# Attention's output product by Strassen's method, with the low parts of its summed weights made by accumulating DMA

## The chip, the cores and the metric

The kernel runs on one core of one Trainium2 chip, as one program. The metric is the device time of one execution in microseconds (us). Before the change the median of three runs is 1040.52 us (1040.29 to 1040.53).

## What is computed

One decoder layer on 512 tokens of width 1024, in float32: a gated feed-forward part, a token mixer, cross-attention into 256 memory tokens, and a second gated feed-forward part, each followed by `x <- LN(alpha*x + sublayer(x))`. The change is in the third, cut here to what matters:

```python
def _memory_attention(h, mem, wq, wk, wv, wo):
    q = (h @ wq).reshape(b_, s_, XA_HEADS, XA_HEAD_DIM)      # 4 heads of 256
    k = (mem @ wk).reshape(b_, m_, XA_HEADS, XA_HEAD_DIM)
    v = (mem @ wv).reshape(b_, m_, XA_HEADS, XA_HEAD_DIM)
    s = jnp.einsum('bshd,bmhd->bhsm', q, k).astype(jnp.float32) * (XA_HEAD_DIM ** -0.5)
    p = jax.nn.softmax(s, axis=-1).astype(v.dtype)
    o = jnp.einsum('bhsm,bmhd->bshd', p, v).reshape(b_, s_, D_MODEL)
    return o @ wo                                            # 512x1024 @ 1024x1024
h = _layernorm(ALPHA * h + _memory_attention(...), ln3_g[l], ln3_b[l])
```

## The kernel before

Every float32 product is made of three matmuls on halves of the numbers: a tile is split into `hi` (a cast on ACT, L67) and `lo` (a subtraction on DVE, L68; the helper is `split`), and hi*hi, hi*lo and lo*hi are added up in PSUM. A weight block of 128 x 1024 (512 KB) is loaded by SP into `raw_...`, split into `whi_...` and `wlo_...` (helper `wblock`; kept blocks are called `ws_...`), and used by all token tiles.

The two feed-forward parts use Strassen's method: 7 products of half-sized matrices instead of 8. The sums of activations that it needs are made on DVE, and those of weights, t1 to t4, by DMA in scratch memory ahead of time: POOL issues a plain copy (L281) and then an accumulating DMA (L290). These are put on a list (`todo_behind`) and issued one at a time behind weight blocks as they come by (`one_behind`: a tiny POOL operation `seen`, L322, reads the new block, and the DMA follows it), at a rate set by `pace`; in the second feed-forward part four at a time behind `seen` at L307. POOL also computes the reciprocal root of each layer-norm (`rstd`, L174).

The attention runs head by head: `xq` projects the queries (tiles `pxq`, split to `q`), `scores` makes `sc`, from which DVE takes the maximum (`mx`, L950) and ACT the exponentials (`e`, L956), DVE scales them (L961), `attend` transposes them on TensorE (`pt`) and splits them (`PT`), and `values` multiplies by the memory's values (`po`) and splits the result (`oT`).

The output product with `wo` is the ordinary one: `out_gemm` (named "xo") takes the output's two halves of 512 columns in turn. For each half, each token tile and each of 8 blocks of 128 inputs there are 3 matmuls of 128x512 (L223 to L225, into `xops`): 2 x 4 x 8 x 3 = 192. Each half is added to `h` (L240), with statistics (L243); after the second half a tile is normalised (`ln_tile`, L166 to L180) and transposed on TensorE (`transpose_h`, into `trh`, split to `xoT`, copied to `y`). The second feed-forward part starts with two ordinary column blocks (`f2p`, L56 to L58, from weights `f2g` and `f2u`), and goes on with Strassen products; its first is `f2w` at L547.

The order of each engine's instructions is made by the framework's scheduler from the program, and is fixed when the kernel is built; semaphores make an engine wait for its inputs.

Of the kernel before, what the change touches and what calls it, by code (L numbers as in the profile page):

```python
# [9 lines left out]
F32 = mybir.dt.float32  # L10
# [6 lines left out]
P = 128  # L17
S = 512
# [16 lines left out]
def layer_kernel(ctx: ExitStack, tc: tile.TileContext, a, out):  # L35
# [35 lines left out]
    def wblock(src, name, stay=False):  # L71
        n = src.shape[-1]
        raw = raw4([P, n], f"raw_{name}")
        nc.sync.dma_start(raw, src)
        if stay:
            both = b8([P, 2, n], F32R, f"ws_{name}")
            hi, lo = both[:, 0, :], both[:, 1, :]
        else:
            hi, lo = q4([P, n], f"whi_{name}"), q4([P, n], f"wlo_{name}")
        split(raw, hi, lo)  # L80
        one_behind(hi)
        return hi, lo
# [183 lines left out]
    class Sums:  # L266


        def __init__(self, wsrc, name, kb1, kb2):
            self.w, self.name, self.kb1, self.kb2, self.T = wsrc, name, kb1, kb2, {}  # L270
            self.copies = [(p, b) for some in (("t1", "t3", "t2"), ("t4",)) for b in range(len(kb1)) for p in some]
            self.adds = list(self.copies)

# [51 lines left out]
    def strassen_gemm(groups, S_, alpha, g, b, eps, name, final=False, pre=None, ys=None):  # L325
# [61 lines left out]
        if len(groups) == 1:  # L387
            quarter_["s1"] = [raw4([P, 4, 256], f"{name}s1")]
        else:
            s1 = b8([P, 2, 4, 256], F32, f"{name}s1")  # L390
            s1_ = [sm.tile([P, n, 256], F32, tag="s1", name=f"{name}s1_{n}", bufs=2) for n in (2, 1)]
            quarter_["s1"] = [s1[:, 0], s1[:, 1], *s1_]
# [61 lines left out]
        return [(tiles[k // 2][:, k % 2, 0, :], tiles[k // 2][:, k % 2, 1, :]) for k in range(KT)]  # L454

# [212 lines left out]
    T0 = b8([P, H * S], F32, "T0")  # L668
    pf01 = proj_T2(wf, X1, "pf")
# [7 lines left out]
    sums2 = Sums(a["w2out"], "f2", *FFN_BLOCKS)  # L677
    todo_behind += sums2.actions()
    pace[:] = 0, 2, 3
# [248 lines left out]
    Q, PP, OT = {}, {}, {}  # L928
# [45 lines left out]
    def values(hd, PT):  # L974
        oT = b8([P, 2, 2, S], F32R, f"oT{hd}")
        for j in range(2):
            po = mm_ps("po")
            csl = slice((2 * hd + j) * P, (2 * hd + j + 1) * P)
            for m in range(2):
                mm3(po, VM[m][:, 0, csl], VM[m][:, 1, csl], PT[:, m, 0, :], PT[:, m, 1, :], m == 0, m == 1)  # L980
            split(po, oT[:, j, 0, :], oT[:, j, 1, :])
        OT[hd] = oT
# [8 lines left out]
    xq(3)  # L991
    p1 = attend(1)
# [7 lines left out]
    X3 = out_gemm(a["wo"], KT, lambda k: (OT[k // 2][:, k % 2, 0, :], OT[k // 2][:, k % 2, 1, :]),  # L1000
                  ALPHA, a["ln3_g"], a["ln3_b"], LN_EPS, "xo", ys=ys,
                  pre=lambda: wx.extend(wblock(a["w2in"][u * FT], f"f2{'gu'[u]}0") for u in range(2)))
# [76 lines left out]
```

## Time and profile before

| | before |
|---|---|
| median of 3 runs | 1040.52 us (1040.29 to 1040.53) |
| the profiled execution, its own time | 1040.28 us |
| its span, first to last instruction | 1038.5 us |
| TensorE (PE) busy | 1024.5 us, 99% |
| PE's weight loads (PEld) | 926.9 us, 89% |
| VectorE (DVE) | 830.7 us, 80% |
| ScalarE (ACT) | 508.3 us, 49% |
| GpSimd (POOL) | 137.4 us, 13% |
| clock granted to TensorE, mean | 0.996 of full speed |

All times below are in us from the span's start. PE's busy time runs to the modelled end of a matmul, which overlaps the next one's start, so the distance of starts tells what a matmul costs.

### The profile page before, as it was taken

What the parts mean: (1) busy time and instruction counts of PE and PEld (TensorE: products, weight loads), DVE (VectorE), ACT (ScalarE), POOL (GpSimd) and SP (SyncE); (2) the same over time, 40 slices, a digit from 0 to 9 for tenths busy, and PEclk for the clock granted to TensorE, in tenths of its full rate; (3) what the DMA queues carried; (4) which work ended last, traced back from release to release, by engine and by line L of the source; (5) the groups of instructions that cost most, each with busy time, mean ns of one, the idle gap of its engine ahead of it and who ended that gap; (6) DMA issues with size and microseconds to landing.
All of it is one profiled execution on the core that took longest, in us unless ns stands there. A gap on an engine that the chain in (4) does not pass through costs nothing. (4 is left out here: it accounts for less than half of the span.)

```text
span 1038.5 us, 17839 instructions
## 1 busy us (share of the span) xinstructions
PE 1024.5 (99%) x6898; PEld 926.9 (89%) x6898; DVE 830.7 (80%) x1360; ACT 508.3 (49%) x879; POOL 137.4 (13%) x212
## 2 busy tenths in 40 slices
PE   9999999999999999999999999999999999999995
PEld 8999999998887988879888988889999999988884
DVE  7999888889989645886686356589988888889885
ACT  5566555566644422235324345236555555565731
POOL 0011111215200101002212100110000000025000
PEclk9999999999999999999999999999999999999998
DMA  9375776578966455544819741603333332359761
GB/s 359 130 243 164 220 230 201 144 232 263 285 212 241 145 155 150 148 128 131 239 60 339 207 110 61 203 23 123 90 104 124 100 102 86 119 178 241 240 236 68
DMA packets 46148, 177.36 MB, mean 171 GB/s; under 512 B 6512, under 2 KB 7792, under 8 KB 42736
## 3 DMA queue, kind: packets, MB, share of 16 engines
q1 hardware_dynamic: 40176, 130.09, 36.3%
q0 software_dynamic: 5888, 46.14, 18.0%
q8 instruction: 54, 0.88, 0.3%
q14 instruction: 30, 0.25, 0.1%
HBM read 174.11 MB, written 48.23 MB: 214 GB/s over the span
## 5 line engine op out<-in xcount | busy, mean ns | idle before, releaser
L547 PE MATMUL f2u<-xt,qf2s 128*128 128x256 f32 x480 | 60.7, 283 | 0.0
L547 PE MATMUL f1u<-xt,qf1s 128*128 128x256 f32 x480 | 60.7, 283 | 0.0
L547 PEld LDWEIGHTS f1u<-xt,qf1s 128*128 128x128 f32 x480 | 59.0, 192 | 0.0
L547 PEld LDWEIGHTS f2u<-xt,qf2s 128*128 128x128 f32 x480 | 59.0, 192 | 0.0
L174 POOL TENSOR_TENSOR rstd<-ve,mhalf 128x1 f32<-128x1 f32 x16 | 15.6, 973 | 153.9 <-DVE ve L172 153.9
L68 DVE TENSOR_TENSOR wlo_wv<-raw_wv,whi_wv 128x1024 fp32r<-128x1024 f32 x12 | 14.7, 1224 | 23.4 <-PE pq L57 8.5
L547 PE MATMUL f2w<-xoT,qf2a 128*128 128x256 f32 x240 | 32.1, 284 | 0.0
L547 PE MATMUL f1u<-xT,qf1a 128*128 128x256 f32 x240 | 32.1, 283 | 0.0
L547 PE MATMUL f2u<-xoT,qf2a 128*128 128x256 f32 x240 | 32.1, 283 | 0.0
L547 PE MATMUL f1w<-xT,qf1a 128*128 128x256 f32 x240 | 32.1, 284 | 0.0
L307 POOL TENSOR_TENSOR seen<-qf2a,mhalf 128x1 f32<-128x1 f32 x10 | 5.9, 593 | 188.2 <-ACT qf2a L67 188.2
L547 PE MATMUL f1u<-xt,qf1a 128*128 128x256 f32 x240 | 30.7, 284 | 0.0
L547 PE MATMUL f1v<-xt,qf1s 128*128 128x256 f32 x240 | 30.7, 284 | 0.0
L547 PE MATMUL f2v<-xt,qf2s 128*128 128x256 f32 x240 | 30.4, 284 | 0.0
L547 PE MATMUL f1v<-xT,qf1s 128*128 128x256 f32 x240 | 30.4, 283 | 0.0
L547 PE MATMUL f2v<-xoT,qf2s 128*128 128x256 f32 x240 | 30.4, 284 | 0.0
L547 PE MATMUL f2u<-xt,qf2a 128*128 128x256 f32 x240 | 30.4, 283 | 0.0
L547 PEld LDWEIGHTS f1w<-xT,qf1a 128*128 128x128 f32 x240 | 30.3, 192 | 0.1
L547 PEld LDWEIGHTS f2w<-xoT,qf2a 128*128 128x128 f32 x240 | 30.3, 192 | 0.0
L547 PEld LDWEIGHTS f1u<-xT,qf1a 128*128 128x128 f32 x240 | 30.2, 192 | 0.0
L547 PEld LDWEIGHTS f2u<-xoT,qf2a 128*128 128x128 f32 x240 | 30.2, 192 | 0.0
L547 PEld LDWEIGHTS f1u<-xt,qf1a 128*128 128x128 f32 x240 | 29.6, 192 | 0.1
(435 smaller groups left out, 3305.8 us busy)
## 6 DMA issues: line engine op xcount, KB each, us to landing
f1t<-in_w1out POOLq DMA_DIRECT2D x30, 512.0 KB, 8.0
f2t<-in_w2out POOLq DMA_DIRECT2D x30, 512.0 KB, 6.6
raw_f1t<-f1t SPq DMA_DIRECT2D x20, 512.0 KB, 4.4
raw_f2t<-f2t SPq DMA_DIRECT2D x20, 512.0 KB, 4.9
raw_f2g<-in_w2in SPq DMA_DIRECT2D x17, 512.0 KB, 3.7
raw_f2u<-in_w2in SPq DMA_DIRECT2D x17, 512.0 KB, 3.8
raw_f1u<-in_w1in SPq DMA_DIRECT2D x15, 512.0 KB, 5.9
raw_f1b<-in_w1out SPq DMA_DIRECT2D x15, 512.0 KB, 7.5
```

The lines of the kernel that those rows point to most:

```text
L68: nc.vector.tensor_tensor(out=lo, in0=src, in1=hi.bitcast(F32), op=ALU.subtract)
L174: nc.gpsimd.tensor_tensor(out=rstd, in0=ve, in1=mhalf[:, 0:1], op=ALU.pow)
L307: ins = nc.gpsimd.tensor_tensor(out=seen, in0=q[:, 0, 0:1].bitcast(F32), in1=mhalf[:, 0:1], op=ALU.mult).ins
L547: nc.tensor.matmul(o, q[:, w, wsl], x[k][r], start=opens and k == 0 and n == 0, stop=ends and k == 3 and n == 2, skip_group_check=True)
```

## The change

The output product goes to a new function `strassen_heads`: 7 products of 256 x 512 x 512, so 7 x 24 = 168 matmuls of 128x512 (L496), into the accumulators u, v and w, two tiles each. The inputs are no longer split as they leave `values`: ACT copies `po` as float32 into two tiles `oT` (L1095), which are split a quarter at a time (`left`, 4 x 256 elements; seven such), with four combinations on DVE (`combine`, L481). The weights: three direct quarters b11, b21, b22 (six blocks, split as before) and four sums t1 to t4 (eight blocks, loaded from scratch). For the sums DVE makes no low part: ACT casts the block to hi (L82) and writes -hi into lo (L83), and POOL issues a DMA that accumulates the float32 source into lo (L84). t1 and t2 are loaded and made behind the last queries, t3 and t4 within the product. 14 additions to `h` (L513, L516) stand in place of 8. The scratch sums of `wo` (8 copies and 8 accumulations, `xot`) are put on the list ahead of those for the second feed-forward part (`f2t`), and the list starts with the mixer's f projections; it is stopped while the product runs, so what is left of f2t goes to the steps of the second feed-forward part.

```diff
-    def wblock(src, name, stay=False):
+    def wblock(src, name, stay=False, by_dma=False):
...
-        split(raw, hi, lo)
+        if by_dma:
+
+            nc.scalar.copy(out=hi, in_=raw)
+            nc.scalar.activation(lo, hi.bitcast(F32), AF.Copy, scale=-1.0)
+            nc.gpsimd.dma_start(lo, src, accum_op=ALU.add, max_dma_last_dim=8192)
+        else:
+            split(raw, hi, lo)
         one_behind(hi)
...
+    def sum_blocks(S_, name, *which):
+
+        for p in which:
+            for i in range(2):
+                assert (p, i) in S_.T and (p, i) not in S_.adds
+                S_.ready[p, i] = wblock(S_.T[p, i], f"{name}{p}{i}", True, True)
+
+    def strassen_heads(A1, A2, S_, alpha, g, b, eps, name, ys=None, fill=None, pre=None):
...
+        A["s1"] = raw4([P, 4, 256], f"{name}s1")
+        product(left("a11"), "b11", u, True)
+        combine("s1", "a21", "a22", ALU.subtract)
+        L = left("s1")
+        for t in range(2):
+            add(t, 0, u[t], True)
+        product(L, "t1", v, True)
+        combine("a21", "a11", "a21", ALU.subtract)
+        combine("a11", "s1", "a11", ALU.subtract)
+        L = left("a11")
+        for t in range(2):
+            add(2 + t, 1, v[t], True)
+        product(L, "t2", u)
+        L = left("a12")
+        for t in range(2):
+            add(t, 1, u[t], True, ALU.subtract)
+        product(L, "b21", w, True, True)
+        combine("a12", "a12", "a11", ALU.add)
+        L, L3 = left("a12"), left("a21")
+        for t in range(2):
+            add(t, 0, w[t], False, last=True)
+        B22 = list(right("b22"))
+        sum_blocks(S_, name, "t3", "t4")
+        L4, T3, T4 = left("a22"), list(right("t3")), list(right("t4"))
+        GB = ln_bcast(g, b)
+        for t in by_tiles(L, B22, v, True):
+            add(t, 1, v[t], False, last=True)
+            ln_tile(t, stats[t], GB, eps)
+        for t in by_tiles(L3, T3, u):
+            add(2 + t, 1, u[t], False, ALU.subtract, last=True)
...
+        if fill is None:
+            transpose_h(0, tiles, ys)
+        for t in by_tiles(L4, T4, u, True):
+            if fill is None and t == 0:
+                transpose_h(1, tiles, ys)
+            add(2 + t, 0, u[t], True, last=True)
+            ln_tile(2 + t, stats[2 + t], GB, eps)
+            if t == 0 and pre is not None:
+                pre()
...
+        for t in range(0 if fill is not None else 2, NT):
+            transpose_h(t, tiles, ys)
...
+    sums_xo = Sums(a["wo"], "xo", [0, 1], [2, 3])
+    sums2 = Sums(a["w2out"], "f2", *FFN_BLOCKS)
+    todo_behind += sums_xo.actions() + sums2.actions()
+    pace[:] = 0, 2, 3
     pf01 = proj_T2(wf, X1, "pf")
...
-    sums2 = Sums(a["w2out"], "f2", *FFN_BLOCKS)
-    todo_behind += sums2.actions()
-    pace[:] = 0, 2, 3
...
-            split(po, oT[:, j, 0, :], oT[:, j, 1, :])
-        OT[hd] = oT
+            nc.scalar.copy(out=OT[hd // 2][:, 2 * (hd % 2) + j, :], in_=po)
...
     xq(3)
+    pace[:] = 0, 0, 1
+    sum_blocks(sums_xo, "xo", "t1", "t2")
     p1 = attend(1)
...
-    X3 = out_gemm(a["wo"], KT, lambda k: (OT[k // 2][:, k % 2, 0, :], OT[k // 2][:, k % 2, 1, :]),
-                  ALPHA, a["ln3_g"], a["ln3_b"], LN_EPS, "xo", ys=ys,
-                  pre=lambda: wx.extend(wblock(a["w2in"][u * FT], f"f2{'gu'[u]}0") for u in range(2)))
+    pace[:] = 0, 0, 1
+    X3 = strassen_heads(*OT, sums_xo, ALPHA, a["ln3_g"], a["ln3_b"], LN_EPS, "xo", ys=ys,
+                        pre=lambda: wx.extend(wblock(a["w2in"][u * FT], f"f2{'gu'[u]}0") for u in range(2)))
```

The first place is ACT while the last queries and the softmaxes of heads 2 and 3 run (`q_6553` and `q_6558` are the last head's queries, `PT_6627` and `PT_6652` the transposed weights of head 1). Before, ACT's rows are

```order
L67 CAST oT_6534<-po 128x512 x2
L67 CAST q_6553<-pxq 128x512
L67 CAST whi_xo_2_6894<-raw_xo_2_6892 128x1024
L67 CAST q_6553<-pxq 128x512
L67 CAST PT_6627<-pt 128x512 x2
L67 CAST whi_xo_3_6904<-raw_xo_3_6902 128x1024
L956 ACTIVATE e,sume<-sc,mx 128x256 x4
L67 CAST oT_6688<-po 128x512 x2
```

and after

```order
L1095 COPY oT_6541<-po 128x512 x2
L67 CAST q_6558<-pxq 128x512
L82 CAST ws_xot_6630<-raw_xot_6628 128x1024
L82 CAST ws_xot_6636<-raw_xot_6634 128x1024
L83 ACTIVATE ws_xot_6630<-ws_xot_6630 128x1024
L83 ACTIVATE ws_xot_6636<-ws_xot_6636 128x1024
L82 CAST ws_xot_6642<-raw_xot_6640 128x1024
L82 CAST ws_xot_6648<-raw_xot_6646 128x1024
L67 CAST q_6558<-pxq 128x512
L83 ACTIVATE ws_xot_6642<-ws_xot_6642 128x1024
L83 ACTIVATE ws_xot_6648<-ws_xot_6648 128x1024
```

Two casts of `wo` blocks have gone from here to a later place, and eight passes over summed weights of the same size have come in ahead of the casts of head 1's `PT`, the last two queries' halves among them. Behind this, the three matmuls of the output product that stood between the first two of the last `po` before (L223 to L225) are no longer there on PE.

The second place is PE at the end of the output product, where the tiles are transposed (trh00 and trh01 are the two halves of token tile 0, trh10 and trh11 those of tile 1). Before, around tile 0:

```order
L223 MATMUL xops11_7073<-whi_xo1_3_6988,oT3_6802 128x512
L224 MATMUL xops11_7073<-wlo_xo1_3_6989,oT3_6802 128x512
L192 MATMUL trh00_7057<-ident_262,h0_266 128x128 x4
L225 MATMUL xops11_7073<-whi_xo1_3_6988,oT3_6802 128x512
L192 MATMUL trh01_7065<-ident_262,h0_266 128x128 x4
L223 MATMUL xops11_7073<-whi_xo1_3_6988,oT3_6802 128x512
L224 MATMUL xops11_7073<-wlo_xo1_3_6989,oT3_6802 128x512
L225 MATMUL xops11_7073<-whi_xo1_3_6988,oT3_6802 128x512
```

and after, where tile 1 is transposed (tile 0 stands just ahead of these rows, tiles 2 and 3 further on among the `f2p`):

```order
L496 MATMUL xou0_6842<-ws_xot40_7027,xoa22_7037 128x512 x6
L496 MATMUL xou0_6842<-ws_xot41_7033,xoa22_7037 128x512 x6
L496 MATMUL xou1_6843<-ws_xot40_7027,xoa22_7037 128x512 x6
L496 MATMUL xou1_6843<-ws_xot41_7033,xoa22_7037 128x512 x5
L198 MATMUL trh10_7153<-ident_262,h1_267 128x128 x4
L496 MATMUL xou1_6843<-ws_xot41_7033,xoa22_7037 128x512
L56 MATMUL f2p0_7256<-xoT0_7120,whi_f2g0_7183 128x256
L56 MATMUL f2p1_7257<-xoT0_7120,whi_f2u0_7189 128x256
L56 MATMUL f2p0_7366<-xoT0_7120,whi_f2g1_7356 128x256
L198 MATMUL trh11_7161<-ident_262,h1_267 128x128 x4
```

Before, three of the four tiles are transposed inside the output product, each a tile's matmuls (24) after the one ahead of it; now tile 1's transposes stand at its last matmul and the first `f2p`, and tiles 2 and 3 come in the `f2p`.

The third place is POOL, from the last DMA of the attention to the layer-norm. Before:

```order
L322 TENSOR_TENSOR seen<-ws_xo_1_6974,mhalf 128x1
L281 DMA f2t_6979<-in_w2out 16x8192
L322 TENSOR_TENSOR seen<-whi_xo_3_6988,mhalf 128x1
L290 DMA f2t_6411<-in_w2out 128x512
L322 TENSOR_TENSOR seen<-whi_f2g_7001,mhalf 128x1
L281 DMA f2t_7007<-in_w2out 16x8192
L174 TENSOR_TENSOR rstd<-ve,mhalf 128x1 x4
```

and after:

```order
L297 DMA f2t_6092<-in_w2out 64x2048
L84 DMA ws_xot_6630<-xot_4121 128x1024
L84 DMA ws_xot_6636<-xot_4263 128x1024
L84 DMA ws_xot_6642<-xot_4227 128x1024
L84 DMA ws_xot_6648<-xot_4556 128x1024
L84 DMA ws_xot_7015<-xot_4159 128x1024
L84 DMA ws_xot_7021<-xot_4459 128x1024
L84 DMA ws_xot_7027<-xot_4815 128x1024
L84 DMA ws_xot_7033<-xot_5056 128x1024
L180 TENSOR_TENSOR rstd<-ve,mhalf 128x1 x4
```

Three pairs of `seen` and an f2t DMA (and some ahead of these rows) have moved to the second feed-forward part, and eight accumulating DMAs into SBUF (L84) stand without any `seen` ahead of the four `rstd` of the layer-norm.

## Rows read from the trace of the kernel before

**Rows 1.** The page: busy time of each engine, its share of the span, instructions.

```profile
PE 1024.5 (99%) x6898; PEld 926.9 (89%) x6898; DVE 830.7 (80%) x1360; ACT 508.3 (49%) x879; POOL 137.4 (13%) x212
```

**Rows 2.** The chain that ended last, by engine.

```profile
PE 32%; DVE 1%; DMA 1%; issue 0%; ACT 0%; DVEq 0%
```

**Rows 3.** Windows: busy time of each engine and instructions, granted clock, DMA share, GB/s.

```profile
626.00:644.00 18.00, 17.76 (x113) 15.55 (x112) 12.81 (x31) 10.43 (x28) 0.56 (x2) 1.00 0.25 88
644.00:694.00 50.00, 49.50 (x229) 40.45 (x230) 33.56 (x51) 13.64 (x19) 8.06 (x11) 1.00 0.33 106
694.00:720.00 26.00, 25.97 (x215) 25.57 (x214) 23.92 (x40) 14.49 (x25) 0.99 (x1) 1.00 0.35 123
```

**Rows 4.** One stretch inside the output product, its matmuls alone (same columns).

```profile
648.00:677.00 29.00, 29.00 (x130) 24.03 (x129) 3.43 (x5) 1.00 0.57 182
```

**Rows 5.** Output product's tile: duration min/median/max, first, last start (L224, L225 alike).

```profile
L223 PE MATMUL xops<-whi_xo,oT x40: 388/390/479, 644.4 to 693.2; 128*128 128x512 f32 x40
L223 PE MATMUL xops<-ws_xo,oT x24: 389/390/398, 668.5 to 690.9; 128*128 128x512 f32 x24
```

**Rows 6.** Groups of instructions by form: busy us, mean ns | idle before.

```profile
L68 DVE TENSOR_TENSOR wlo_xo<-raw_xo,whi_xo 128x1024 fp32r<-128x1024 f32 x3 | 3.7, 1226 | 8.0 <-PE xops L224 4.3 <-PE pxq L57 3.7
...
L67 ACT CAST ws_xo<-raw_xo 128x1024 fp32r<-128x1024 f32 x3 | 3.1, 1058 | 0.0
...
L68 DVE TENSOR_TENSOR oT<-po,oT 128x512 fp32r<-128x512 f32 x6 | 3.9, 685 | 1.9 <-ACT oT L67 1.9
...
L240 DVE SCALAR_TENSOR_TENSOR h<-h,xops 128x512 f32<-128x512 f32 x8 | 5.5, 684 | 4.3 <-PE xops L225 4.3
L747 ACT ACTIVATE mg<-pm,psc x4: 692/692/693, 435.6 to 461.2; 128x512 fp32r<-128x512 f32 x4
```

**Rows 7.** Timeline of ACT: start, duration, [idle before it <- what ended it].

```profile
629.55 0.59 ACT L67 CAST q<-pxq 128x512 fp32r<-128x512 f32 x1 [3.85 <-PE pxq L58]
630.04 1.07 ACT L67 CAST PT<-pt 128x512 fp32r<-128x512 f32 x2
```

**Rows 8.** Timeline of PE where the values end.

```profile
643.87 0.73 PE L56 MATMUL po<-PT,VM 128*128 128x512 f32 x2 [0.24 <-ACT PT L67]
644.44 0.40 PE L223 MATMUL xops<-whi_xo,oT 128*128 128x512 f32 x1
```

**Rows 9.** Timeline of PE at the first and at the last token tile's transposes.

```profile
678.23 0.39 PE L224 MATMUL xops<-wlo_xo,oT 128*128 128x512 f32 x1
679.12 0.63 PE L192 MATMUL trh<-ident,h 128*128 128x128 f32 x4 [0.50 <-DVE h L180]
...
700.33 0.28 PE L58 MATMUL f2p<-xoT,wlo_f2g 128*128 128x256 f32 x1
700.63 0.63 PE L192 MATMUL trh<-ident,h 128*128 128x128 f32 x4
```

**Rows 10.** POOL's accumulating DMAs (L290): time to issue one; from issue to landing.

```profile
L290 POOL DMA_DIRECT2D f2t<-f2t x12: 763/796/854, 420.9 to 956.7; - x12
DMA to landing us min/median/max: 4.3/7.1/9.5
```

**Rows 11.** Timeline of POOL and DVE late in the second feed-forward part.

```profile
936.42 6.92 POOL L322 TENSOR_TENSOR seen<-whi_f2t,mhalf 128x1 f32<-128x1 f32 x1 [0.69 <-ACT whi_f2t L67]
...
944.22 0.78 POOL L290 DMA_DIRECT2D f2t<-f2t  x1
...
942.08 1.22 DVE L347 TENSOR_TENSOR f2g<-f2s,f2g 128x1024 f32<-128x1024 f32 x1
...
944.15 1.22 DVE L68 TENSOR_TENSOR f2a<-f2g,f2a 128x1024 fp32r<-128x1024 f32 x1
```

**Rows 12.** The first Strassen product of the second feed-forward part (its tile): first and last start.

```profile
L547 PE MATMUL f2w<-xoT,qf2a x240: 282/284/284, 718.3 to 901.1; 128*128 128x256 f32 x120
```

**Rows 13.** Windows inside the first and the second feed-forward part.

```profile
100.00:150.00 50.00, 50.00 (x419) 50.00 (x419) 43.77 (x82) 29.50 (x56) 9.64 (x15) 1.00 0.68 196
800.00:850.00 50.00, 50.00 (x419) 50.00 (x419) 42.83 (x79) 27.72 (x55) 1.26 (x2) 1.00 0.41 132
```

More of the change, by code (lines that the diff above doesn't have):

```diff
@@ L272, in __init__ @@
             self.adds = list(self.copies)
+            self.ready = {}
         def copy(self, behind):
@@ L386, in strassen_gemm @@
         L = left("a11")
[L387 to L392, printed above, removed]
+        s1 = b8([P, 2, 4, 256], F32, f"{name}s1")
+        s1_ = [sm.tile([P, n, 256], F32, tag="s1", name=f"{name}s1_{n}", bufs=2) for n in (2, 1)]
+        quarter_["s1"] = [s1[:, 0], s1[:, 1], *s1_]
         product(L, "b11", u, True)
@@ L927, in layer_kernel @@
             split(ps[t], VM[t][:, 0, sl], VM[t][:, 1, sl])
-    Q, PP, OT = {}, {}, {}
+    Q, PP, OT = {}, {}, []
     def xq(hd):
@@ L974, in values @@
     def values(hd, PT):
-        oT = b8([P, 2, 2, S], F32R, f"oT{hd}")
+        if hd % 2 == 0:
+            OT.append(b8([P, 4, S], F32, f"oT{hd // 2}"))
         for j in range(2):
```

48 lines of the change are left out of this document (added).

## The prediction

> **What bounds the kernel now.** The page comes first: PE is busy 99% of the span, DVE 80%, ACT 49% [rows 1], and the chain that ended last is PE at nearly every step that it names [rows 2]. So time is won by taking matmuls away, and lost wherever PE is made to wait. The windows around the change come next [rows 3]: from 644 to 694, the output product, PE has 0.50 idle, the clock is granted in full (1.00, the 2.4 GHz level), and DVE is busy 33.6 of 50, ACT 13.6. From 626 to 644, the softmaxes of the last heads, PE has 0.24 idle, DVE is busy 12.8 of 18 and ACT 10.4. The reader is to see that the product is a PE stretch with room on DVE and ACT, and that the softmaxes ahead of it are a chain over three engines in which PE is kept busy only by what the order puts in between.
>
> **What is taken away.** In a stretch inside the product 130 matmuls start in 29.00 us and PE is never idle: 129 distances of start to start, so 0.225 us each [rows 4]. 192 of them (40 and 24 of each of three lines [rows 5]) become 168. The saving is 24 x 0.225 = 5.4 us, which is 0.52% of the time. No other engine's saving counts.
>
> **What DVE and ACT get.** Taken away on DVE: eight subtractions of `po` (0.69 each) and two of weight blocks (1.23, six left of eight). Added: seven splits of 4 x 256 elements (1.23, the same form), four combinations (no row of this shape and source here; both inputs in SBUF as in the weight subtraction, so 1.2), six more additions to h (0.68) [rows 6]. That is -5.5 - 2.5 + 8.6 + 4.9 + 4.1 = +9.6, so DVE comes to some 43 us in what will be about 46: it still fits, with little room. On ACT a summed block needs two passes of 1.06 (the cast has its row; the negation, an ACTIVATE with a scale, took 0.69 on half the elements where a cast takes 0.59, so between 1.06 and 1.4; I take 1.1 as the fixed part is paid once) [rows 6]. Sixteen passes are 17 us, half of them between 624 and 644, half inside the product, where ACT was idle 36 of 50 [rows 3].
>
> **Ahead of the product: the softmaxes.** This is the first dear place. In the ACT rows eight passes, 8.6 us, now stand ahead of the casts of head 1's `PT`, while two weight casts (2.1) leave. Before, ACT had been idle 3.85 until 629.55, and cast `PT` from 630.04 [rows 7]. The passes can begin when the ACT work of 624 is done, so they fill that hole and push the casts to about 633: 3 late. PE does not feel all of that, since 24 scores of head 2, some 2.9 us of work, stand between the transposes and `po`. But DVE keeps its order: the lo parts of `PT` now stand between the two maxima of head 2, so the second exponential, the scaling, and after it the same chain for head 3, each come later, and at head 3 nothing is left for PE to do but wait. Before, PE waited 0.24 there for ACT's `PT`, and then filled with three matmuls of the product (644.44) what was still missing [rows 8]; those are no longer ready at that place, as the product's first split comes after `PT`. Walking the three engines' orders with the durations above, the product's first matmul comes at 648.8, where the same work with before's waits would have put it at 646.7. **+2.1.** Bounds: 0.5 if the scores hide nearly all, 3.8 if the 3.1 of the late cast passes in full and the 0.7 of the lost fill with it.
>
> **Inside the product.** Each product is 24 matmuls, 5.4 us, and six follow one another before the first transposes. The tightest step is the first: s1 needs the last `po` (ACT copy 0.6, subtraction 1.2, cast 1.06 beside the second combination 1.2, lo 1.2: 4.5 us after it) against 5.4 of the first product: 0.9 to spare. All others have 1 to 6 us in the walk. I put 0, covered by the product ahead; a slip of 1 us on DVE beyond that cover would be paid as it is.
>
> **The accumulating DMAs into SBUF** (L84, POOL) have no row. The nearest are L290's, in memory: 0.8 to issue, 4.3 to 9.5 from issue to landing, median 7.1 [rows 10]. t1 and t2 are issued some 20 us ahead of their use: hidden. t3's follow ACT's negations, which end in my walk at 667.6 and 668.6 and are wanted at 676.2 and 677.6; t4's 671.3 and 672.3 against 682.5 and 683.8. Margins 8.6 to 11.5 against a median of 7.1 and a worst of 9.5: **0**, bounds 0 and 0.9 by those rows, and more only if SBUF as a target is worse than they are.
>
> One behaviour of POOL speaks against this. Its operation `seen`, on one column, took 6.92 at 936.42 and ended at 943.34, as a run of DVE subtractions with both inputs in SBUF ended (942.08 + 1.22). The DMA issue after it was not held: 0.78 at 944.22, beside the next such subtraction of 944.15 [rows 11]. The Trainium skill says, in "GPSIMD Engine Reference", section 1 (Specifications), that GpSimd shares its SBUF interfaces with VectorE and contends with DVE instructions that have two SBUF inputs; the trace agrees for `seen`, and not for the issue of a DMA. By the row the sum stays as it is; by the rule, if issuing were held as `seen` was, it would be 1039.4 (rival 2).
>
> **Behind the product: transposes and layer-norm.** Before, PE loses 0.66 at the first transposes (679.12 - 678.23 - 0.23), which wait for the normalised h, and 0.18 at a late one (700.63 - 700.33 - 0.12) [rows 9]; these are the first and the last but one of eight, the others lose about 0.1 each, so 1.4 in all. In the new order DVE makes the layer-norms of tiles 0 and 1 while it also adds up h for tiles 2 and 3, and tile 1's first transposes wait for a PSUM buffer that tile 0's evacuation (ACT, behind a DVE subtraction queued after the layer-norm) still holds: 0.6. The first `f2p` then waits for a split on ACT behind the cast of a weight block: 1.25. Six further transposes lose 0.9. Together 2.8 against 1.4: **+1.4.** Bounds: -0.7 (the 0.66 of now gone too, nothing new), +3 (DVE, now nearly full, brings the last tile's layer-norm 1.5 later than the first half of `f2p` covers).
>
> **The second feed-forward part** gets 16 more scratch DMAs from the list. In the first part, which runs the same program beside its own sums, the DMA share is 0.68 and PE is busy 50.00 of 50; in the second it is 0.41 now [rows 13]: 0, hidden as there. The last sums are issued later, but during the product of b21, and t4's is read two products of 15 us (66 matmuls) on.
>
> **The sum.** -5.4 + 2.1 + 0 + 1.4 = -1.9: the first `f2w`, at 718.3 now [rows 12], comes at about 716.4, and nothing behind it changes. Against the profiled execution's 1040.28 that is 1038.4; that execution lies 0.24 under the median of the runs, which I leave inside the rounding.
>
> **Rivals.**
> 1. *The full saving.* The waits ahead of and behind the product are hidden by orders that the walk takes too strictly, say 0.5 and 0: 1040.3 - 5.4 + 0.5 = 1035.4, or anything up to 1037. For it: PE idles only 0.5 now in the whole product [rows 3]. Against it: the lost fill and the four passes of ACT in front of `PT` stand in the order. Chance 0.18.
> 2. *Late DMAs: the slower side.* t3 and t4 land after PE wants them, because the accumulation into SBUF is slower than that in memory, or its issue is held as `seen` was. PE waits, and the layer-norms of tiles 2 and 3 behind it. Each us of landing beyond 8.6 is a us of time. Held by DVE's longest such run in the new order there (two operations, 2.5 us), a median DMA lands after 9.6: 1039.4. From 12.7 on, when 4.1 are added, the kernel is slower by over 2 us: 1042.5 and more. For it: no such DMA has been seen, and up to seven loads run beside these four. Against it: 48 accumulations, none above 9.5 [rows 10]. Chance 0.2, of it 0.1 slower.
> 3. *DVE or ACT becomes the bound.* The softmax delay passes in full (3.8 for 2.1: 1040.1) or the last layer-norm slips (3 for 1.4: 1040.0), or both (1041.7); a slip of 1 us inside the product besides makes it slower than before by over 2. For it: DVE at 43 of 46. Against it: each has cover in the walk. Chance 0.13, of it 0.04 slower.
>
> My own forecast, 1037 to 1039.6, has the other 0.49.
>
> **How the numbers follow.** The time is that of the likeliest, 1038.4. 0.2% of this time is 2.1 us, about what a measurement can tell from no change, so the forecast lies on the edge: half of its chance is faster, half the same. Faster: 0.25 + 0.18 = 0.43. Slower: 0.1 + 0.04 = 0.14. Same: the 0.43 that are left. The range reaches into rival 1 to 1036.0 and over 2 and 3 to 1041.5.
>
> **What will show it.** 168 matmuls at L496, 0.225 apart; the first of them at 648.8 (646.7 would refute the softmax term); waits of PE for `PT` of 1 to 2 us around 636 to 646; no wait of xou or xov for a DMA or POOL; L84 landing in under 8.6; trh10 and the first `f2p` waiting for ACT, 0.6 and 1.25; `f2w` at 716.4. Wrong it would be above all if PE waits inside the seven products, where I have put nothing.

## The result, and the profile after

The changed kernel takes 1043.3 us (median of 9 runs, 1042.1 to 1046.24) against 1040.63 of the kernel before (9 runs, 1040.02 to 1041.94) on the same chip: a ratio of 1.0028 [1.0018, 1.0039], so 0.28% slower. The forecast of 1038.4 had the wrong sign.

The profiled execution of after is its fastest run: 1042.1, with a span of 1040.3 against 1038.5. What is taken apart below is therefore 1.8 us of the 2.7 between the medians. The page's busy times and three windows of after, for [rows 1] and [rows 3]:

```profile
PE 1020.7 (98%) x6874; PEld 922.5 (89%) x6874; DVE 835.0 (80%) x1367; ACT 526.6 (51%) x900; POOL 164.6 (16%) x234
```

```profile
626.00:644.00 18.00, 17.61 (x108) 14.86 (x106) 8.84 (x24) 14.09 (x32) 3.46 (x4) 1.00 1.03 260
644.00:694.00 50.00, 46.69 (x216) 37.55 (x216) 42.83 (x61) 27.80 (x35) 5.39 (x6) 1.00 0.57 159
694.00:720.00 26.00, 26.00 (x215) 25.73 (x216) 25.82 (x42) 15.14 (x26) 1.98 (x2) 1.00 0.26 82
```

PE is busy 3.8 us less, and yet the program is longer. In the product's window PE now idles 3.3 of 50 where it idled 0.5. The waits of PE, summed by what they wait for, name it (the 1.1 of L109 stood in before too):

```profile
PE xou L496 <- DMA ws_xot<-xot: 2.1, 2, 1.2
PE idle L109 <- DVE mhalf L163: 1.1, 1, 1.1
PE f2w L374 <- DVE wlo_f2b L68: 0.8, 1, 0.8
PE po L56 <- ACT PT L67: 0.6, 1, 0.6
PE pt L1082 <- DVE e L1074: 0.5, 2, 0.3
PE f2p L56 <- ACT xoT L67: 0.4, 1, 0.4
```

The accumulating DMAs that the forecast had put at nothing are the largest new wait. (A row names the waiting tile, what it waits for, the sum in us, the number of waits and the longest.) Yet the second feed-forward part still starts early. The matmuls of `xou` and of `f2w` in after, with first and last start (for the first Strassen product of [rows 12], L659 is L547 of before):

```profile
L496 PE MATMUL xou<-whi_xob,xoa x16: 389/389/395, 648.6 to 653.8; 128*128 128x512 f32 x16
...
L659 PE MATMUL f2w<-xoT,qf2a x240: 283/283/283, 717.4 to 900.2; 128*128 128x256 f32 x120
L374 PE MATMUL f2w<-whi_f2b,f2a x44: 387/389/503, 964.1 to 980.4; 128*128 128x512 f32 x44
```

`f2w` comes at 717.4 for 718.3: 0.9 won there. PE's last matmul starts at 1026.30 for 1026.46. So up to PE's end the profiled execution is still slightly ahead, and the 1.8 us is lost behind the last matmul. What ends the program are the `DRAIN` rows, which stand behind the last work in each engine's queue. POOL's and SP's, before and then after (duration min/median/max in ns, first and last start), with POOL's last `rstd` of after:

```profile
L1075 POOLq DRAIN  x3: 40/93/8944, 1028.8 to 1038.2; - x3
L1075 SPq DRAIN  x3: 7/7/7, 1033.5 to 1038.0; - x3
```

```profile
L1190 POOLq DRAIN  x3: 46/102/10909, 1028.6 to 1040.0; - x3
L1190 SPq DRAIN  x3: 7/7/7, 1033.5 to 1039.8; - x3
...
1028.65 0.99 POOL L180 TENSOR_TENSOR rstd<-ve,mhalf 128x1 f32<-128x1 f32 x1 [5.36 <-DVE ve L178]
```

Of POOL's three, the long one is the first. Its row starts as the last `rstd` starts (1028.6 and 1028.65 in after), so it holds the 0.99 of that as well. SP, which stores the output, reaches its first drain at 1033.5 in both. It then stands until POOL's long drain is over: 1028.8 + 8.94 = 1037.7 before, 1028.6 + 10.91 = 1039.5 after. So both programs end on a wait for POOL, and after's is 1.97 longer.

The budget of the profiled execution, after minus before, from the starts in the traces ("the product" is its first matmul). First `pxq` matmul: -0.08 (575.68 for 575.76). From there to the product: +1.92 (72.89 for 70.97; before's product counted from 646.73: it went on at 647.41, with three of its matmuls, 0.68, already done). Product to first `f2w`: -2.79 (68.83 for 71.62). From there to the last matmul: +0.79. Drain: +1.97. Together +1.8.

### The profile page after: what moved, and what is told of

Its sections match the earlier page's. It is cut to its first block, busy times and chain, and to the rows that moved or that the text cites. A ratio compares the mean times of both kernels' runs of the same rounds, so it can differ in the third digit from the quotient of the medians.

```text
span 1040.3 us, 17867 instructions
## 1 busy us (share of the span) xinstructions
PE 1020.7 (98%) x6874; PEld 922.5 (89%) x6874; DVE 835.0 (80%) x1367; ACT 526.6 (51%) x900; POOL 164.6 (16%) x234
## 4 chain that ended last, share of the span: by engine, by line
PE 90%; issue 4%; DMA 3%; ACT 1%; DVE 1%; DVEq 0%; POOL 0%; ACTq 0%; POOLq 0%
PE f1u L659 11%; PE f2u L659 11%; PE f1u L374 6%; PE f1v L659 6%; PE f2v L659 6%; PE f2u L374 4%; PE f2v L374 3%; PE f1v L374 3%; PE f2w L659 3%; PE f1w L659 3%; PE f1w L374 1%; PE mops L230 1%; PE mops L229 1%; PE mops L231 1%; DMA ws_xot<-xot 1%
## 5 line engine op out<-in xcount | busy, mean ns | idle before, releaser
L659 PE MATMUL f1u<-xt,qf1s 128*128 128x256 f32 x480 | 60.7, 283 | 0.0
L659 PE MATMUL f2u<-xt,qf2s 128*128 128x256 f32 x480 | 60.7, 283 | 0.0
L659 PEld LDWEIGHTS f1u<-xt,qf1s 128*128 128x128 f32 x480 | 59.0, 192 | 0.0
L659 PEld LDWEIGHTS f2u<-xt,qf2s 128*128 128x128 f32 x480 | 59.0, 192 | 0.0
L314 POOL TENSOR_TENSOR seen<-qf1a,mhalf 128x1 f32<-128x1 f32 x10 | 5.6, 556 | 179.3 <-ACT qf1a L67 136.9
L68 DVE TENSOR_TENSOR wlo_wv<-raw_wv,whi_wv 128x1024 fp32r<-128x1024 f32 x12 | 14.7, 1224 | 23.3 <-PE vps L878 8.4
L659 PE MATMUL f1u<-xT,qf1a 128*128 128x256 f32 x240 | 32.1, 283 | 0.0
L659 PE MATMUL f2w<-xoT,qf2a 128*128 128x256 f32 x240 | 32.1, 283 | 0.0
L659 PE MATMUL f2u<-xoT,qf2a 128*128 128x256 f32 x240 | 32.1, 283 | 0.0
L659 PE MATMUL f1w<-xT,qf1a 128*128 128x256 f32 x240 | 32.1, 283 | 0.0
L659 PE MATMUL f1u<-xt,qf1a 128*128 128x256 f32 x240 | 30.7, 283 | 0.0
L659 PE MATMUL f1v<-xt,qf1s 128*128 128x256 f32 x240 | 30.6, 283 | 0.0
L659 PE MATMUL f1v<-xT,qf1s 128*128 128x256 f32 x240 | 30.4, 283 | 0.0
L659 PE MATMUL f2v<-xt,qf2s 128*128 128x256 f32 x240 | 30.4, 283 | 0.0
L659 PE MATMUL f2v<-xoT,qf2s 128*128 128x256 f32 x240 | 30.4, 283 | 0.0
L659 PE MATMUL f2u<-xt,qf2a 128*128 128x256 f32 x240 | 30.4, 283 | 0.0
L659 PEld LDWEIGHTS f1w<-xT,qf1a 128*128 128x128 f32 x240 | 30.3, 192 | 0.1
L659 PEld LDWEIGHTS f1u<-xT,qf1a 128*128 128x128 f32 x240 | 30.2, 192 | 0.0
L659 PEld LDWEIGHTS f2w<-xoT,qf2a 128*128 128x128 f32 x240 | 30.2, 192 | 0.0
L659 PEld LDWEIGHTS f2u<-xoT,qf2a 128*128 128x128 f32 x240 | 30.2, 192 | 0.0
```

The source lines that it names most:

```text
L68: nc.vector.tensor_tensor(out=lo, in0=src, in1=hi.bitcast(F32), op=ALU.subtract)
L314: ins = nc.gpsimd.tensor_tensor(out=seen, in0=q[:, 0, 0:1].bitcast(F32), in1=mhalf[:, 0:1], op=ALU.mult).ins
L659: nc.tensor.matmul(o, q[:, w, wsl], x[k][r], start=opens and k == 0 and n == 0, stop=ends and k == 3 and n == 2, skip_group_check=True)
```

## The experiments

The theory after this reading: POOL's long drain grows with the number of DMAs that POOL has issued, and the accumulations land late because they are slow in themselves. The rivals: the new wait at `f2w` for b21 (0.8 in the table above) follows from POOL's `seen`, held 13.54 us there for 6.92 in [rows 11]; the late landing is only a matter of late issue, or of too many transfers at once. Ratios below are to the kernel before on the same chip, with a 95% interval.

**The sums alone.** The kernel before, with the 16 scratch DMAs of `wo` on the list and nothing that uses them (matmuls as before):

```diff
+    sums_xo = Sums(a["wo"], "xo", [0, 1], [2, 3])
+    sums2 = Sums(a["w2out"], "f2", *FFN_BLOCKS)
+    todo_behind += sums_xo.actions() + sums2.actions()
+    pace[:] = 0, 2, 3
     pf01 = proj_T2(wf, X1, "pf")
...
-    sums2 = Sums(a["w2out"], "f2", *FFN_BLOCKS)
-    todo_behind += sums2.actions()
-    pace[:] = 0, 2, 3
...
     xq(3)
+    pace[:] = 0, 0, 1
```

> The kernel before with one part of the change alone: the 16 scratch DMAs that sum wo (xot) go on the list ahead of the f2t ones and the list is stopped where the change stops it; the sums are not used, the output product stays the ordinary one. Theory (the change lost its gain in three places: the late sums t3 and t4, a later weight load in the last product because the f2t sums are shifted, and POOL's last DRAIN, which lasts 8.94 us before and 10.91 after, 0.082 us more for each of 24 more POOL DMAs): the drain lasts 8.9 + 16 x 0.082 = 10.3, the last product waits some 0.8 as after the change, so 1040.6 + 1.3 + 0.8 = 1042.7 us. Rival (the drain and the end do not depend on the number of POOL DMAs, all is lost in the output product): 1040.6 us, drain 8.9.

Measured: 1041.55 (11 runs), 1.001 [1.0001, 1.0019]. Its drain:

```profile
L1077 POOLq DRAIN  x3: 40/93/10251, 1028.4 to 1039.1; - x3
```

10.25 for 112 DMAs, 1.31 more than the 8.94 for 96. PE ended 0.42 earlier than in before and the span was still 0.9 longer. The cost of the drain stands without the change to the product. The wait for b21 was not there, so the sums alone don't make it; the 1042.7 expected had counted it in.

**Low parts by DVE in place of accumulating DMA**, for t3 and t4, for all four sums, and for t1 and t2 alone:

```diff
-    def sum_blocks(S_, name, *which):
+    def sum_blocks(S_, name, *which, by_dma=True):
...
-                S_.ready[p, i] = wblock(S_.T[p, i], f"{name}{p}{i}", True, True)
+                S_.ready[p, i] = wblock(S_.T[p, i], f"{name}{p}{i}", True, by_dma)
...
-        sum_blocks(S_, name, "t3", "t4")
+        sum_blocks(S_, name, "t3", "t4", by_dma=False)
...
-    sum_blocks(sums_xo, "xo", "t1", "t2")
+    sum_blocks(sums_xo, "xo", "t1", "t2", by_dma=False)
```

The first call alone (t3, t4):

> The changed kernel with the low parts of t3 and t4 made by DVE's subtraction instead of ACT's negation and an accumulating DMA. Theory (accumulating DMAs into SBUF hold the DMA engines for twice as long as a load, beside five loads of f2 weights, and land 6.6 to 14.2 us after issue): the two waits of xou for the DMA, 2.1 us, vanish, and the drain is 4 x 0.082 = 0.3 shorter: 1043.3 - 2.4 = 1040.9 us. Rival (DVE, with 4 x 1.22 more in the stretch before the layer-norms, is the next bound): the wait moves to DVE's splits or to the transposes, 1042.5 to 1044 us.

Both calls:

> The changed kernel with all four sums split by DVE: no negation on ACT, no DMA into SBUF; the 16 scratch DMAs stay. Theory: as with t3 and t4 alone, and the drain 8 x 0.082 = 0.7 shorter than after the change; ACT has 4 passes less ahead of head 1's PT, so PE's delay of 1.85 us in the softmaxes falls to 1 or less, DVE having room there: 1043.3 - 2.1 - 0.7 - 0.9 = 1039.6 us. Rival (the softmax chain is set by DVE, which gets 4 x 1.22 more in that stretch): the first xou no earlier than 648.5, 1040.5 us or more.

The second call alone (t1, t2):

> The changed kernel with t1 and t2 split by DVE, t3 and t4 kept with negation and accumulating DMA. Theory: the softmax term falls from 1.9 to 0.4 as in dve_all (ACT's four negations gone from ahead of PT), the waits of xou for the DMA of t3 and t4 stay at 2.1 to 2.5, drain 4 x 0.082 = 0.3 shorter: 1.8 us below the changed kernel timed beside it. Rival (the softmax term is due to the accumulating DMAs' traffic on SBUF or to the order of PE alone): first xou no earlier after the first pxq than 72.5 us, no gain beyond 0.3.

Measured: 1040.79 (1.0004 [0.9995, 1.0013]), 1039.08 (0.9986 [0.9977, 0.9995]), 1039.58 (0.9987 [0.9977, 0.9996]). From the first `pxq` matmul to the product they take 72.88, 71.32 and 71.36 us, against 72.89 in after. So the delay ahead of the product, 1.92, falls to 0.35 and 0.39 where t1 and t2 are split by DVE, and only there. The casts stay on ACT in these runs and with a plain DMA (below) the 72.89 stays. So what costs 1.5 is ACT's four negations of t1 and t2, half of the eight passes of the forecast. From the product to `f2w` they take 68.97, 68.98 and, with t3 and t4 still by DMA, 69.54 (646.92 to 716.46). With t3 and t4 on DVE the wait for the DMA is gone and PE waits for DVE; the waits of PE with all four there:

```profile
PE xou L496 <- DVE h L516: 1.3, 1, 1.3
...
PE f2p L58 <- DVE wlo_f2g L68: 0.7, 1, 0.7
PE f2p L57 <- DVE xoT L68: 0.3, 1, 0.3
```

With t1 and t2 alone on DVE the first of those places still reads:

```profile
PE xou L496 <- DMA ws_xot<-xot: 2.8, 2, 1.8
```

So for t3 and t4 the DMA against DVE is a draw in that stretch (DVE is 0.56 better where it splits t1 and t2 too), and for t1 and t2 DVE is better by 1.5 us. That t3 and t4 on DVE came out at the 1040.9 of the theory was luck: the wait moved to DVE, as the rival had said, and what the trace gains on after's, 2.0 us, lies between `f2w` and the last matmul (306.9 for 308.9), where the wait for b21 is missing. The drains follow the DMAs left on POOL, 10.58 with 116 and 10.26 with 112 (of the 0.33 saved with 116 the end of the program shows little: 13.98 and 14.13 from the last matmul for 14.02, as 0.3 to 0.4 more stands behind the long drain there); for t3 and t4 on DVE:

```profile
L1190 POOLq DRAIN  x3: 46/102/10584, 1027.5 to 1038.9; - x3
```

**A plain DMA in place of the accumulating one**, with the same source, target and size. This kernel leaves out the addition, so its low parts hold the sum itself; the edit drops a limit on the transfer's pieces too, but the four DMAs move in 576 packets either way:

```diff
-            nc.gpsimd.dma_start(lo, src, accum_op=ALU.add, max_dma_last_dim=8192)
+            nc.gpsimd.dma_start(lo, src)
```

> The changed kernel with the eight DMAs of L84 as plain loads into lo (no accumulation, so the low parts are wrong: lo holds the sum itself); everything else, the number of POOL's DMAs too, is kept. Theory (an accumulating DMA into SBUF holds the DMA engines for about 2.7 us of all 16 where a load of the same size takes 1.4, so four of them and five weight loads fill 20 us): landing 4 to 8 us after issue instead of 6.6 to 14.2, xou waits for no DMA, first f2p some 2 us earlier relative to the first xou: 40.8 instead of 42.8 us. Rival (POOL's issue, or SBUF as the target of a POOL DMA, is what is slow, accumulating or not): landing stays at 10 us and the 2.1 us of waits stay. The drain stays at 10.9 either way: 1041 to 1043 us.

Measured: 1040.43 (10 runs), 0.9998 [0.9989, 1.0007]. Issue to landing, and the window in which t3 and t4 are fetched (last two numbers: DMA share and GB/s), first in after:

```profile
L84 POOL DMA_DIRECT2D ws_xot<-xot x8: 848/857/884, 627.8 to 672.1; - x8
...
DMA to landing us min/median/max: 6.6/11.0/14.2
```

```profile
667.00:687.00 20.00, 17.85 (x82) 14.22 (x81) 16.54 (x28) 8.26 (x10) 5.39 (x6) 1.00 0.95 257
```

and here:

```profile
DMA to landing us min/median/max: 5.4/6.9/8.4
```

```profile
667.00:687.00 20.00, 20.00 (x94) 16.62 (x93) 17.97 (x30) 8.63 (x11) 4.14 (x6) 1.00 0.72 258
```

The same bytes in the 20 us, but the DMA engines are busy 0.95 with accumulation and 0.72 without, and PE's idle time in the window goes from 2.15 to 0. From the product to `f2w` it is 66.65: 2.18 less than after. POOL's issue falls too, from 0.86 to 0.54 us each, which is too little to make up the landing times. So the accumulation itself is the cost, not the number of transfers. The queues divide so (packets, MB, share of 16 engines' time), in after's window and, last, here:

```profile
q0 software_dynamic: 576, 2.10, 54.4%
q1 hardware_dynamic: 838, 3.04, 40.9%
...
q0 software_dynamic: 576, 2.10, 30.6%
```

Queue 0 holds the four accumulations: 10.9 us of all 16 engines, 2.7 for each 512 KB, and 1.5 as plain DMAs. Queue 1 holds loads: 8.2 us for 3.04 MB, so 1.4 for 512 KB.

Is SBUF as the target to blame? The kernel before shows what an accumulation in scratch memory takes. Queue 0 in two windows of it that hold one such DMA (L290) each, 615 to 621 and 444 to 452:

```profile
q0 software_dynamic: 80, 0.52, 50.0%
...
q0 software_dynamic: 80, 0.52, 34.9%
```

That is 3.0 and 2.8 us of all 16 engines for 512 KB, so no less than into SBUF. The wait for b21 (0.8) and the long `seen` were here too, so the accumulations don't cause those.

**t3 and t4 issued one product earlier:**

```diff
             add(2 + t, 1, v[t], True)
+        sum_blocks(S_, name, "t3", "t4")
         product(L, "t2", u)
...
-        sum_blocks(S_, name, "t3", "t4")
         L4, T3, T4 = left("a22"), list(right("t3")), list(right("t4"))
```

> The changed kernel with t3 and t4 loaded, cast, negated and accumulated before the product with t2 instead of after that with b21, at a time when the DMA engines moved next to nothing (646 to 654: share 0.00). Theory (t3 and t4 were late because their accumulations shared the DMA engines with five loads of f2 weights): no wait of xou for a DMA, -2.1 us; some of it comes back as waits for DVE at the transposes (up to 1): 1041.2 to 1042.2 us. Rival (the passes on ACT, now ahead of the b21 blocks, delay these): PE waits for whi or wlo of xob at the products with b21 and b22, 1043 us or more.

Measured: 1042.92, 1.002 [1.0012, 1.0029]: the rival was right in its mechanism, and nearly in its number. The DMA wait is gone, but ACT makes its eight passes for t3 and t4 (655.7 to 663.3) ahead of its casts of wo's direct block b21, for which PE then waits. The timeline of PE there:

```profile
665.29 0.73 PE L496 MATMUL xow<-whi_xob,xoa 128*128 128x512 f32 x2 [0.31 <-ACT whi_xob L67]
667.34 0.50 PE L496 MATMUL xow<-wlo_xob,xoa 128*128 128x512 f32 x1 [1.31 <-DVE wlo_xob L68]
667.67 0.93 PE L496 MATMUL xow<-whi_xob,xoa 128*128 128x512 f32 x2
668.40 0.63 PE L496 MATMUL xow<-wlo_xob,xoa 128*128 128x512 f32 x1
668.83 0.63 PE L496 MATMUL xow<-whi_xob,xoa 128*128 128x512 f32 x1
669.26 0.63 PE L496 MATMUL xow<-wlo_xob,xoa 128*128 128x512 f32 x1
...
672.94 0.39 PE L496 MATMUL xow<-wlo_xob,xoa 128*128 128x512 f32 x1
673.17 0.61 PE L496 MATMUL xow<-whi_xob,xoa 128*128 128x512 f32 x2
```

After the stalls the matmuls start 0.43 apart (668.40, 668.83, 669.26) and later 0.23 again. The granted clock over 667 to 687 is 0.91, and 0.66 over 667 to 672, with part of that at the lower level of 1.2 GHz. So the order buys off one wait and pays others: from the product to `f2w` it takes 71.71, 2.9 more than after.

**The drain taken off the end.** The last feed-forward's layer-norms take their reciprocal square root on ACT and DVE, so POOL has nothing left to do at the end, in the kernel before, in after, and with all sums on DVE:

```diff
-    def ln_tile(t, stats, GB, eps):
+    def ln_tile(t, stats, GB, eps, on_act=False):
...
-        nc.gpsimd.tensor_tensor(out=rstd, in0=ve, in1=mhalf[:, 0:1], op=ALU.pow)
+        if on_act:
+            nc.scalar.activation(ve, ve, AF.Sqrt)
+            nc.vector.reciprocal(rstd, ve)
+        else:
+            nc.gpsimd.tensor_tensor(out=rstd, in0=ve, in1=mhalf[:, 0:1], op=ALU.pow)
...
-            ln_tile(t, stats[t], GB, eps)
+            ln_tile(t, stats[t], GB, eps, final)
```

> The kernel before with the last layer-norm's reciprocal root off POOL, nothing else. Theory (POOL's drain of 8.94 us for 96 DMAs sets the end of this kernel too, 4.4 us after SP's last step at 1033.6): 1040.5 - 4.2 = 1036.3 us; then the whole product change with splits on DVE is worth more than the 1.4 us that it showed, since its 16 more DMAs cost nothing: dve_all_rstd 2.5 us below this one. Rival (before, the drain was short enough to be hidden behind the last outputs): 1040.5 us.

> The changed kernel with the reciprocal root of the last layer-norm made by ACT (square root) and DVE (reciprocal) instead of POOL, so that POOL's last operation is the last f2t accumulation, near 975. Theory (POOL's DRAIN at the end starts when POOL has nothing left, lasts some 11 us by the number of its DMAs, and sets the end of the program, 6 us after the last output has landed): it starts near 975, is hidden, and the program ends some 0.5 us after SP's last step at 1033.6: 1043.3 - 6 = 1037.3 us. Rival (the DRAIN waits for the other engines, or its length is not set by POOL's DMAs): no change, 1043.3 us.

> All four sums split by DVE, and the last layer-norm's reciprocal root off POOL. Theory (the two savings add up: dve_all ended 5.5 us after its last output was out, 1036.59 against 1030.8 plus 0.3 that any program has): 1039.1 - 5.3 = 1033.8 us, the shortest of all. Rival (the square root on ACT lengthens the last chain or its table load meets the casts of the last weights, as the later last matmul of after_rstd, 1029.3 against 1026.3, could mean): 1036 to 1037 us.

Measured: 1036.32 (0.9958 [0.9946, 0.9971]), 1039.11 (0.9984 [0.9974, 0.9993]) and 1035.17 (0.9949 [0.9935, 0.9962]). All are faster than the same kernel with POOL's `rstd`: by 4.2 us, by 3 to 4 (after was 1043.3 and, timed again below, 1041.97) and by 3.9. After missed its 1037.3, and is still 2.8 us behind before here: its trace is 2.8 us longer between `f2w` and the last matmul (310.39 for 307.57), with the wait for b21 (0.8) in it. The third missed its 1033.8. A new wait stands in its trace, which is of its slowest execution, 1037.04:

```profile
PE f2u L378 <- DVE wlo_f2t L68: 1.9, 1, 1.9
```

The cast that this wait goes back to is the second of these rows of ACT:

```profile
1004.74 1.04 ACT L67 CAST ws_f2t<-raw_f2t 128x1024 fp32r<-128x1024 f32 x1 [2.89 <-DMA raw_f2t<-f2t]
1005.69 0.61 ACT L67 CAST whi_f2t<-raw_f2t 128x512 fp32r<-128x512 f32 x1
```

It stood in ACT's order behind a cast that waited 2.89 for a load. The square roots of token tiles 0 and 1 had been done by 1001.9. So what cost here was this order, with a late load; that ACT stood before the square roots, as was thought at the time, the trace does not show. With only the last two tiles' roots moved (`final and t > 1`):

> The kernel before with the reciprocal root of the last two token tiles alone off POOL (tiles 0 and 1 keep POOL, so that ACT does not stand before their statistics while the casts of the last weights wait behind it). Theory: POOL's last operation is near 1003, its drain of 9 to 11 us ends before the last output is out: 1036 us, as with all four tiles. Rival: the table load of the square root, now at tile 2, lies on the last chain: 1037.5 us.

> The changed kernel, accumulating DMAs and all, with the reciprocal root of the last two token tiles off POOL, so that its drain is hidden and ACT does not stand before tiles 0 and 1. Theory (the drain is the constant part of the loss): the kernel before with the same edit took 1036.1 to 1038.1, median 1036.75; this one -0.2 to -1 us at its best and up to 2 above where the last product waits for DMA: 1036 to 1038 us; against the kernel before as it is, 3 to 5 us faster. Rival (the output product of this change is itself slower): above 1038 us.

> All four sums split by DVE, and the reciprocal root of the last two token tiles off POOL. Theory (the 1.9 us wait of the last product for wlo_f2t in dve_all_rstd came from ACT, which stood before the square root of tiles 0 and 1 with the casts of weights behind it): that wait goes, last matmul near 1023.5 to 1024, 1033.5 us. Rival (the drain hidden, the last product's DMAs set it): 1035 us as with all four tiles.

Measured: 1036.75 (0.9962 [0.9949, 0.9976]), 1035.48 (0.9943 [0.9927, 0.9959]) and 1034.1 (0.9934 [0.992, 0.9947]; one of its five executions took 5321.88, for no known reason, and is not in the ratio). In the third the cast named above comes at 998.08, ahead of the one that waits for the load, and the wait of 1.9 is gone. The drains of after in this form:

```profile
L1194 POOLq DRAIN  x3: 46/93/10914, 1004.2 to 1034.8; - x3
L1194 SPq DRAIN  x3: 7/7/7, 1034.3 to 1034.6; - x3
```

POOL's long drain is as long as ever, 10.91, but starts at 1004.2, and the program ends 0.8 behind SP's first drain instead of 6.8 (1040.3 - 1033.5). From the start of the last matmul to the end it is now 8.10 in after and 7.96 in before, where it was 14.02 and 12.04. That settles it: the drain's length was on the path. With it hidden in this way, after is no longer seen behind before (0.9943 against 0.9962, the intervals overlapping, each against the kernel before on its own chip), and the version with all four sums on DVE is the fastest of the study, 0.66% under the kernel before.

**The changed kernel again**, with no edit: two single executions, then a timing of twelve.

> The changed kernel again, for a second profile of it, since its executions lie between 1042.1 and 1046.2 us and the profile at hand is of the fastest. Theory (POOL's operation seen is held for 13.5 us by DVE's run of subtractions in the last product, the scratch DMAs that it holds back bunch up with the loads of b21's blocks, and PE waits for these): seen lasts 13.5 at some 935, the loads of raw_f2b land 10 us or more after issue, PE waits for b21, and a slower execution has more of that. Rival: the seen is short here, and the slower executions lose their time in the output product (t3 and t4 later still).

> The changed kernel a third time, with the same two readings as the second.

> The changed kernel once more, timed in five rounds beside the kernel before on another occasion. Theory (the constant part of its loss is the drain, 2.0 us, less 0.2 to 1 us that its last matmul comes earlier, and what lies above that is DMA landing late in the last product in some executions): 0.5 to 3 us above before, no execution below before's lowest by over 1 us, a spread of 3 us or more where before has 2. Rival (a constant slower product): always 2.5 us above.

Measured: 1041.34, 1041.19 (before beside them 1041.05, 1040.79 to 1041.72) and 1041.97 (12 runs, 1039.82 to 1043.8), 1.0009 [0.9998, 1.0019]. The spread of 3 us or more showed (4.0), but before had 5.1 beside it, so it tells nothing. PE's wait for the accumulations was 2.5, 2.3 and 2.2 us in these, much as the 2.1 above. The wait for b21 is not constant. The 66 matmuls of b21 (44 `whi`, 22 `wlo`) start over 16.3 us in the profiled execution of after (964.1 to 980.4 above), and in the first of these over 14.8:

```profile
L374 PE MATMUL f2w<-whi_f2b,f2a x44: 389/389/395, 964.5 to 979.3; 128*128 128x512 f32 x44
```

`seen` was held 13.5 us in that one too. A long `seen` without the wait: held alone, it does not make the wait. What does differ is how long the loads of `raw_f2b`, the blocks that b21's product needs, take from issue to landing, in after and in this execution:

```profile
DMA to landing us min/median/max: 2.5/5.8/13.2
...
DMA to landing us min/median/max: 2.5/5.4/11.6
```

In the four traces in which the matmuls of b21 start over 16.2 to 16.9 us (after, its two forms with roots moved, and the plain DMA) the longest of these loads takes 13.0 to 13.7; in the thirteen others it takes 11.8 or less, and the matmuls start over 14.7 to 15.0. All four have a `seen` of 13.5, behind which five DMAs of POOL start at 949.0 to 956.3 (in after), beside the first of these loads.

## Why the prediction was wrong

**The step that failed** is "the first `f2w`, at 718.3 now [rows 12], comes at about 716.4, and nothing behind it changes". Something did change: POOL's drain at the end, +1.97. The forecast counted 24 more DMAs on POOL and asked only whether their transfers were hidden. The row of before that carries the cost, a drain of 8.94 us at the program's end, was not looked at. Rows of four lengths put the price at 0.082 each: 8.94 with 96 DMAs, 10.25 with 112, 10.58 with 116, 10.91 with 120, and 1.97 / 24 = 0.082. All 24 move 512 KB, so a price by bytes would look the same; a price by packets would not: the 16 for `wo`'s sums moved 56 each, the eight accumulations 144 each, at the same 0.082.

**"The accumulating DMAs into SBUF ... 0"** failed too. L290's rows were taken as the nearest, with a median of 7.1 [rows 10]; L84 landed after 11.0 at the median and up to 14.2 where t3's margin was some 8.6. They were issued when the walk had said (667.4 to 672.1). PE waited 2.1, which the plain DMA took back (2.18). The rival of late DMAs had named this wait, by the reason "slower than that in memory", and the traces do not bear that out: an accumulation in memory holds the DMA engines as long (3.0 and 2.8 above, for 2.7). Its other reason, an issue held as `seen` was, did not happen: the issue took 0.86, near L290's 0.80 [rows 10], also at 667.39, beside a subtraction of weights on DVE (1.23 from 667.59). The rule of the Trainium skill that had been weighed there ("GPSIMD Engine Reference", section 1, Specifications) thus left the issue of these DMAs alone, as [rows 11] had said. Beside t3 and t4 run some six weight loads of the next part (the 3.04 MB of queue 1), and each accumulation holds the DMA engines twice as long as a load: together 19 of the 20 us of that window. Of L290's 48 never more than three were in flight, and mostly one. So it was four at once beside loads that came late, and a median landing taken from elsewhere could not show it. The forecast had noted the loads ("up to seven loads run beside these four"), and yet gave the case a chance of 0.2. That rival's time, 1042.5 and more, was near the measured one by luck: its own mechanism gave 2.2, which is 1040.6.

**The softmaxes, +2.1**, were right: +1.92, and by the mechanism given, ACT's passes ahead of `PT`, as DVE splitting t1 and t2 shows. The product's first matmul was forecast at 648.8 and came at 648.6.

**The matmuls, -5.4**: 168 starts at L496, 0.23 apart, as forecast.

**Behind the product, +1.4**, was too much. With a plain DMA the stretch from the product to `f2w` is 4.97 shorter than before, so only 5.4 - 4.97 = 0.4 is left for all that was priced there. The first `f2p` waited for ACT 0.4 in after and 1.0 with a plain DMA, for the 1.25 of the forecast, and no `trh` waited 0.6.

Put together: -5.4 + 1.9 + 2.2 + 0.4 = -0.9 at `f2w`, as measured (717.4 for 718.3; the 0.4 is what was left over, so this closes by itself), for a forecast of -1.9. Behind it +0.8 and +2.0.

**What stays open.** The +0.79 between `f2w` and the last matmul is the wait for b21's blocks, whose product takes 1.6 us longer than before's (16.3 for 14.7), less 0.8 that before lost in its last product and after did not. That wait comes in some executions (after, with a plain DMA, and after with the roots moved) and not in others of the same kernel. Neither the sums alone, the accumulations, nor a long `seen` alone makes it; it came where `seen` was long and the loads of b21's blocks took 13 us or more. Why they take 11.6 in one execution and 13.2 in another was not found. It may be part of why after was 1.0028 in one comparison and 1.0009 in another; this was not shown. That after is not faster holds in both. How much slower, between 0.1% and 0.3%, is not settled better than that.

## What to carry to other kernels

Look at what ends the program, not only at what ends the work. Here it was POOL's drain, which ended 4 to 6 us after SP had done its last step, so every DMA added to that queue anywhere in the kernel was paid for at the end; giving POOL's last operation to other engines was worth more than the change. A DMA that accumulates should be priced by the DMA engine time it holds and by what runs beside it, not by the median landing of another stretch. Work taken from a busy engine costs where the next engine stands in a chain: the same low parts made ahead of the product cost 1.9 us through ACT and 0.4 through DVE.

## What the runs showed of the hardware

- POOL's drain at the program's end took 0.082 us more for each DMA (of 512 KB) that POOL had issued in the whole program, and not only for late ones: the 16 copies and sums of `wo` and the eight accumulations, the last of which was issued at 672.1, cost alike. Its row begins with POOL's last `rstd` and holds the 0.99 of it. What is left behind that is 7.92 with 96 DMAs and 9.89 with 120, 0.082 each and nothing else. Where POOL finished at 1004, it took the same 10.91. In the three forms with all roots moved the row began at 957 to 977 and took 10.89, 11.88 and 21.19; the last began at 970.6 while POOL still held a `seen` until 978.3 and issued two DMAs behind it. From the last issue it was 9.98, 10.95 and 11.82 in these, 1 to 3 us more than behind an `rstd`; why was not found.
- A 512 KB accumulation took 2.7 us of all 16 DMA engines into SBUF, and 2.8 and 3.0 in scratch memory; a plain DMA of POOL 1.5, a load by SP 1.4.
- POOL's `seen`, on one column, took 13.5 us at its longest in the profiled execution of after, 13.5 and 9.2 in the two single executions; PE waited for b21 in the first of these three only.
- After stalls of 0.31 and 1.31 the granted clock dropped to the lower level and matmuls ran 0.43 apart for some 3 us; the waits of 1.19 and 0.96 in after, some 8 us apart, left the clock at 1.00.
